# A graph attention layer on one core: program order throughout, half of the one-hot transposes by DMA, block loads on GpSimd's queue, the last scaling on ScalarE

## The chip, the cores and the metric

The kernel runs on one core of one Trainium2 chip. The metric is the device time of one execution in microseconds; before the change it is 372.82 us, the median of three runs (372.75 to 373.14).

## The reference

4096 nodes with 64 features, 50,000 directed edges, 4 heads, 64 output features per head. Cut to what matters:

```python
x_proj[h] = x @ weight[h]
score[h, e] = sum(x_proj[h, src[e]] * att_src[h]) + sum(x_proj[h, dst[e]] * att_dst[h])
score = where(score > 0, score, 0.2 * score)
output[h, dst[e]] += exp(score[h, e]) * x_proj[h, src[e]]      # for every edge
output[h, n] /= sum(exp(score[h, e]) for e with dst[e] == n) + 1e-8
return output.transpose(1, 0, 2).reshape(num_nodes, -1)
```

## The kernel before

The edges are first brought into order by two sorts on VectorE, so that afterwards each block of 121 destination nodes finds its edges in 16 groups of at most 128, one group for each sixteenth of the source nodes. Then 34 blocks are worked off, with one-hot matrices in place of gathers and scatters.

**First sort** (L529 to L546). The edges lie as 128 rows of 391. VectorE makes a key from source and destination, sorts the rows and then runs of 8 rows (`Sorter.rows`, `Sorter.runs`, nearly all of it L183), and SyncE stores the result to DRAM (`store`, L237). Beside it ScalarE counts with 16 Sign passes how many keys lie below each boundary (`below`, L245). `tables` (L298) stands behind the store: it loads x and the weights, transposes x on PE, multiplies it with the attention vectors (at_ps, L335), and keeps in `xa` each node's features and its attention terms, in `adb` the terms of the destinations. `bounds` (L251) adds up the counts on PE (L256) and turns them on VectorE (L258 and following) into the addresses at which the second stage reads.

**Second sort** (`group`, L286). GpSimd gathers runs from DRAM by these addresses (L283), VectorE sorts again, SyncE stores, `bounds` gives the addresses of the blocks' windows. `Windows` gathers them, five pieces of 8 blocks each, and `unpack` (L352) splits each piece on VectorE into destination and source index and writes both as bf16 to DRAM (`gat_bins`), two stores a piece on SyncE. `longest` finds the longest run of edges; at the very end of the program every engine loads the two lengths into registers (L559, L561) and branches on them (L563). With this input the branch's body doesn't run.

**Blocks** (`Blocks.run`, L454). For block b, in program order of one turn of the loop:

- `load(b+3)`, on SyncE: 1 MB, the indices of a block, the same for all 128 partitions. Three buffers.
- `weigh(b)`, VectorE: wv, the larger of the two exponentials (L433), and val = xs x wv (L437).
- `gather(b+1)`, PE: 48 products of one-hot matrices with `xa` and `adb`; ScalarE then takes the exponentials (ex, L410) and the features (xs, L412) out of PSUM.
- `turn(b+1)`, PE and ScalarE: 16 transposes of the destinations' one-hot matrix into PSUM (L425), two copies of 8 back to SBUF (Sb, L426).
- `onehot(b+2)`, VectorE: the block's indices compared with the partition number, two operations (L390, L391).
- `give(b-1)`: PE multiplies the sums with the weights (pf, L490), VectorE adds 1e-8, takes the reciprocal and scales (inv, res, L493 to L496), SyncE stores the result (L499).
- `scatter(b)`, PE: 48 products, for each of 16 groups two with val and one with wv, into acc; ScalarE copies acc (aT, L483).

Sb, the one-hots, val, ex, xs and wv have two buffers each; xps, acc and pf have one. Each engine, and each DMA queue, works in the order in which its instructions are issued. From L525 on this is the order of the program (`manual_schedule`); the setup ahead of it (L61 to L142) is ordered by the scheduler.

Of the kernel before, what the change touches and what calls it, by code (L numbers as in the profile page):

```python
# [9 lines left out]
P = 128  # L10
# [3 lines left out]
I32 = mybir.dt.int32  # L14
# [21 lines left out]
def kernel(ctx: ExitStack, tc: tile.TileContext, x: bass.AP, edge_index: bass.AP,  # L36
# [25 lines left out]


# [43 lines left out]
    pm8 = bits("pm8", 0, 7)  # L107
    goff = cst.tile([P, 1], F32)
# [167 lines left out]

    def fetch(pool, skey, start, n, to, what):
# [63 lines left out]
    NT = NR  # L341

    class Windows:
# [9 lines left out]
        def unpack(self, i):  # L353
# [7 lines left out]
            for k in range(2):  # L361
                nc.sync.dma_start(out=dataclasses.replace(bin_dram[8 * i, k],
                                                          ap=[[2 * NR * W2, 8], [W2, NR], [1, W2]]),
                                  in_=self.tb[:, i, k, :])

    class Blocks:
# [27 lines left out]
        def gather(self, b):  # L394
# [4 lines left out]
            xps = self.psx.tile([P, 4, 512], F32, name="xps")  # L399
            for t in range(NT):  # L400
                o = xps[:, t // 4, (t % 4) * XC:(t % 4) * XC + XC]
# [10 lines left out]
            S.copy(out=xs[:], in_=av(xps[:], 0, [512, 4], [XC, 4], [1, Din]))  # L412
            self.ex[b], self.xs[b] = ex, xs

        def turn(self, b):
# [5 lines left out]
            for q in range(2):  # L421
                sp = self.pss.tile([P, NT // 2, W2], BF16, name="sp")
                for i in range(NT // 2):
                    t = q * NT // 2 + i
                    T.transpose(out=sp[:, i, :], in_=oh[:, 0, t * W2:(t + 1) * W2], identity=identb[:])  # L425
                S.copy(out=Sb[:, q * NT // 2:(q + 1) * NT // 2, :], in_=sp[:])  # L426
            self.Sb[b] = Sb

        def weigh(self, b):
# [7 lines left out]
            V.tensor_tensor(out=av(val[:], 0, [Dout, H], [C, NT], [1, Din]),  # L437
                            in0=av(xs[:], 0, [0, H], [2, NT * Din // 2], [1, 2]),
                            in1=av(wv[:], 0, [2, H * NT], [0, Din // 2], [1, 2]), op=OP.mult)
            self.val[b] = val  # L440

        def scatter(self, b):

            val, wv, Sb = self.val.pop(b), self.wv.pop(b), self.Sb.pop(b)
            acc = self.psa.tile([P, CW], F32, name="acc")
            for t in range(NT):
                for k in range(2):
                    T.matmul(out=acc[:, k * P:(k + 1) * P], lhsT=val[:, t, k * P:(k + 1) * P], rhs=Sb[:, t, :],  # L448
                             start=(t == 0 and k == 0), stop=(t == NT - 1), skip_group_check=True)
                T.matmul(out=acc[:, C:CW], lhsT=Sb[:, t, :], rhs=av(wv[:], 2 * t, [2 * NT, H]), start=False,  # L450
                         stop=(t == NT - 1), skip_group_check=True)
            self.sink.take(b, acc[:])

        def run(self, between=lambda: None):  # L454
            for b in range(3):
                self.load(b)
# [3 lines left out]
            between()  # L460
# [12 lines left out]
    class Finish:  # L473
# [7 lines left out]
        def take(self, b, acc):  # L481
            aT = self.fp.tile([P, CW], F32, name="aT")
            S.copy(out=aT[:], in_=acc)  # L483
# [131 lines left out]
```

## Time and profile before

The profiled execution took 373.68 us, its span 371.9 us.

| stretch, us | what happens | VectorE busy, us |
|---|---|---|
| 0 to 20 | edges land, sort 1 begins | 14.51 |
| 20 to 73 | sort 1 | 50.12 |
| 73 to 90 | x and weights land, tables on PE | 0.00 |
| 90 to 120 | at_ps on PE, then bounds | 2.22 |
| 120 to 164 | sort 2 | 37.37 |
| 164 to 186 | windows, unpack, first block loads | 10.90 |
| 196 to 360 | blocks | 156.74 of 164 |

Over the span PE is busy 58%, VectorE 76%, ScalarE 44%, GpSimd 5%. A timeline row gives the start, the duration, the engine (with q: its queue of issues), the line, the operation and the tiles, and in brackets how long the engine was idle before it and what ended that. Durations of operations that follow each other overlap a little; the distance from start to start is what an engine spends on one.

### The profile page before, as it was taken

The numbers are of one execution on the slowest core, as the hardware profiler recorded it, in microseconds if no ns is written. First come the engines' busy times: TensorE is split into PE (matmuls) and PEld (weight loads), VectorE is DVE, ScalarE is ACT, GpSimd is POOL, SyncE is SP. The second block draws the span as 40 slices with busy tenths as digits, with TensorE's granted clock in tenths as the row PEclk, the third lists the DMA queues.
The fourth block names the chain that finished last, engine by engine and source line by source line (L and its number), as shares of the span: only waits on it lengthen the run. The fifth ranks groups of instructions, "written<-read, shape, count | busy, mean of one in ns | idle before, by whom it ended". The sixth has DMA issues, their size and how long they took to land.

```text
span 371.9 us, 9662 instructions
## 1 busy us (share of the span) xinstructions
PE 215.6 (58%) x4122; PEld 206.5 (56%) x4122; DVE 282.4 (76%) x584; ACT 164.3 (44%) x290; POOL 18.9 (5%) x40
## 2 busy tenths in 40 slices
PE   0000000029996000000399999999999999999990
PEld 0000000016996000000399999999999999999980
DVE  4999999700002599974599999999999999999970
ACT  1840000015000499600086666655765566656640
POOL 2820000000000200014000000000000000000000
PEclk9999999999555555555599999999999999999996
DMA  2000000050000100002866556655675567655410
GB/s 86 1 7 0 0 0 1 28 120 0 2 0 0 29 0 0 1 28 67 345 227 223 199 220 254 239 200 208 245 250 200 205 243 254 209 203 229 143 42 20
DMA packets 13550, 43.96 MB, mean 118 GB/s; under 512 B 3308, under 2 KB 8492, under 8 KB 9148
## 3 DMA queue, kind: packets, MB, share of 16 engines
q1 hardware_dynamic: 12556, 42.22, 32.1%
q0 software_dynamic: 704, 0.66, 0.7%
q8 instruction: 34, 0.56, 0.7%
q10 hardware_dynamic: 240, 0.40, 0.3%
q14 instruction: 16, 0.13, 0.1%
HBM read 38.22 MB, written 5.05 MB: 116 GB/s over the span
## 4 chain that ended last, share of the span: by engine, by line
DVE 60%; PE 25%; DMA 6%; issue 3%; ACT 2%; SPq 1%; POOL 1%; DVEq 0%; POOLq 0%
DVE val L437 14%; DVE sA L183 11%; DVE sB L183 10%; DVE oh L390 7%; PE at_ps L335 7%; PE acc L448 7%; DVE oh L391 4%; PE sp L425 3%; DVE res L496 3%; PE xps L403 3%; DMA wS<-in_weight_dram 2%; PE xps L405 2%; PE pf L490 1%; PE ps L330 1%; DMA bc<-gat_bins 1%
## 5 line engine op out<-in xcount | busy, mean ns | idle before, releaser
L437 DVE TENSOR_TENSOR val<-xs,wv 128x4096 bf16<-128x4096 bf16 x34 | 77.9, 2292 | 4.1 <-ACT xs L412 0.6
L448 PE MATMUL acc<-Sb,val 128*128 128x128 bf16 x1088 | 79.9, 217 | 1.2
L450 PE MATMUL acc<-wv,Sb 128*128 128x4 bf16 x544 | 76.0, 168 | 0.0
L448 PEld LDWEIGHTS <-val 128*128 128x128 bf16 x1088 | 67.2, 96 | 6.3 <-DVE val L437 6.1
L426 ACT COPY Sb<-sp 128x1024 bf16<-128x1024 bf16 x68 | 66.2, 1039 | 0.0
L403 PE MATMUL xps<-xa,oh 128*128 128x72 bf16 x544 | 53.9, 194 | 15.5 <-DVE oh L390 15.5
L403 PEld LDWEIGHTS <-oh 128*128 128x128 bf16 x544 | 50.3, 98 | 15.8 <-DVE oh L390 15.8
L405 PE MATMUL xps<-xa,oh 128*128 128x72 bf16 x544 | 53.7, 195 | 0.4 <-DVE oh L391 0.4
L407 PE MATMUL xps<-adb,oh 128*128 128x8 bf16 x544 | 52.8, 169 | 0.0
L450 PEld LDWEIGHTS <-Sb 128*128 128x128 bf16 x544 | 52.1, 96 | 0.0
L407 PEld LDWEIGHTS <-oh 128*128 128x128 bf16 x544 | 50.2, 97 | 0.0
L405 PEld LDWEIGHTS <-oh 128*128 128x128 bf16 x544 | 49.6, 96 | 0.6 <-DVE oh L391 0.6
L390 DVE TENSOR_SCALAR oh<-bc,pF 128x4096 bf16<-128x4096 bf16 x34 | 43.5, 1281 | 7.0 <-DMA bc<-gat_bins 7.0
L318 PE MATMUL ps<-ident,wS 64*128 64x64 f32 x2 | 0.7, 350 | 80.8 <-DMA wS<-in_weight_dram 80.8
L318 PEld LDWEIGHTS ps<-ident,wS 64*128 64x128 f32 x2 | 0.4, 178 | 80.8 <-issue 80.8
L183 DVE TENSOR_TENSOR sA<-sB 128x256 f32<-128x256 f32 (+2 forms) x108 | 39.7, 409 | 1.8
L410 ACT ACTIVATE ex<-xps 128x128 f32<-128x128 f32 x34 | 9.4, 277 | 65.1 <-PE xps L407 65.1
L183 DVE TENSOR_TENSOR sB<-sA 128x256 f32<-128x256 f32 (+2 forms) x100 | 36.8, 409 | 1.7
L425 PE MATMUL sp<-identb,oh 128*128 128x128 bf16 x544 | 36.6, 221 | 0.0
L258 DVE TENSOR_SCALAR cnt<-cnt_ps 128x17 f32<-128x17 f32 (+1 forms) x3 | 0.5, 180 | 44.8 <-PE cnt_ps L256 44.8
L412 ACT CAST xs<-xps 128x1024 bf16<-128x1024 f32 x34 | 34.2, 1007 | 0.0
L425 PEld LDWEIGHTS <-oh 128*128 128x128 bf16 x544 | 31.5, 99 | 0.0
(115 smaller groups left out, 295.9 us busy)
## 6 DMA issues: line engine op xcount, KB each, us to landing
bc<-gat_bins SPq DMA_DIRECT2D x34, 1024.0 KB
out_dram<-res SPq DMA_DIRECT2D x33, 121.0 KB
gat_sorted<-sA SPq DMA_DIRECT2D x2, 256.0 KB
eD<-in_edge_index_dram ACTq DMA_DIRECT2D x1, 390.0 KB
eS<-in_edge_index_dram SPq DMA_DIRECT2D x1, 390.0 KB
gat_bins<-tb SPq DMA_DIRECT2D x10, 32.0 KB
out_dram<-res SPq DMA_DIRECT2D x1, 103.0 KB
win<-gat_sorted,wi POOLq DMA_INDIRECT x5, 2.5
```

Of the source, the lines that this page charges most:

```text
L183: V.tensor_tensor(out=av(d[:], o, [2 * h, n], [1, h]), in0=av(s[:], 0, [2 * h, n], [1, h]), in1=av(s[:], h, [2 * h, n], [1, h]), op=op)
L335: T.matmul(out=ps[:, b, :], lhsT=xT[:, b * step:b * step + P], rhs=uv[:, k, :], start=(b == 0), stop=True, skip_group_check=True)
L390: V.tensor_scalar(out=oh[:, 0:2, :], in0=bc[:], scalar1=pF[:, 0:1], scalar2=None, op0=OP.is_equal)
L403: T.matmul(out=o, lhsT=oh[:, 1, e], rhs=xa[:, 2 * t, :], start=(t % 4 == 0), stop=False, skip_group_check=True)
L405: T.matmul(out=o, lhsT=oh[:, 2, e], rhs=xa[:, 2 * t + 1, :], start=False, stop=False, skip_group_check=True)
L407: T.matmul(out=o[:, Din:XC], lhsT=oh[:, 0, e], rhs=adb[:, b, :], start=False, stop=True, skip_group_check=True)
L412: S.copy(out=xs[:], in_=av(xps[:], 0, [512, 4], [XC, 4], [1, Din]))
L425: T.transpose(out=sp[:, i, :], in_=oh[:, 0, t * W2:(t + 1) * W2], identity=identb[:])
L426: S.copy(out=Sb[:, q * NT // 2:(q + 1) * NT // 2, :], in_=sp[:])
L437: V.tensor_tensor(out=av(val[:], 0, [Dout, H], [C, NT], [1, Din]), in0=av(xs[:], 0, [0, H], [2, NT * Din // 2], [1, 2]), in1=av(wv[:], 0, ...
L448: T.matmul(out=acc[:, k * P:(k + 1) * P], lhsT=val[:, t, k * P:(k + 1) * P], rhs=Sb[:, t, :], start=(t == 0 and k == 0), stop=(t == NT - 1 ...
L450: T.matmul(out=acc[:, C:CW], lhsT=Sb[:, t, :], rhs=av(wv[:], 2 * t, [2 * NT, H]), start=False, stop=(t == NT - 1), skip_group_check=True)
```

## The change

- `manual_schedule` is entered at the start, so that the setup too stands in program order.
- `tables` is called ahead of the first sort instead of behind its store.
- The run lengths are loaded into registers right after `longest`, by a helper `room`.
- `unpack` takes the queues for its two stores: SyncE and ScalarE for piece 0, ScalarE for the others. The loads of blocks 0 to 2 are issued right after piece 0; all pieces are unpacked before the blocks begin.
- Block loads are issued on GpSimd's queue.
- `turn`: groups 8 to 15 are transposed by one DMA transpose on SyncE, groups 0 to 7 on PE as before, with one copy.
- ex is written as bf16, doubled and in the order in which wv is written; wv then reads it without strides.
- `scatter` makes the 16 products with wv first, then those with val, half by half, and streams 121 columns instead of 128. The last block's val is made in two halves.
- The 1e-8 is added by ScalarE as it copies the sums; the last scaling is four ScalarE activations with the reciprocal as scale.

```diff
+    order = ExitStack()
+    order.enter_context(tc.manual_schedule())
...
+    eps = cst.tile([P, 1], F32)
+    V.memset(eps[:], 1e-8)
...
+    def room(k, n):
+        return nc.values_load(most[0:1, k:k + 1], min_val=0, max_val=RUN * n,
+                              skip_runtime_bounds_check_because="a count of a run's edges")
...
+    NP = NT // 2
+    AW = 2 * BD + H
...
-            for k in range(2):
-                nc.sync.dma_start(out=dataclasses.replace(bin_dram[8 * i, k],
...
+            for k, eng in enumerate(engs):
+                eng.dma_start(out=dataclasses.replace(bin_dram[8 * i, k], ap=[[2 * NR * W2, 8], [W2, NR], [1, W2]]),
...
-                nc.sync.dma_start(out=t[:], in_=dataclasses.replace(bin_dram[b], ap=[[0, P], [NT * W2, 2],
+                nc.gpsimd.dma_start(out=t[:], in_=dataclasses.replace(bin_dram[b], ap=[[0, P], [NT * W2, 2],
...
-            xps = self.psx.tile([P, 4, 512], F32, name="xps")
+            xps = self.psx.tile([P, NT, P], F32, name="xps")
...
-            ex = self.bp.tile([P, NT, 2 * H], F32, name="ex")
-            S.activation(out=ex[:], in_=av(xps[:], Din, [512, 4], [XC, 4], [1, 2 * H]), func=ACTF.Exp)
+            ex = self.bp.tile([P, 2, H, NT, 2], BF16, name="ex")
+            S.activation(out=av(ex[:], 0, [2, NT], [2 * NT, 2 * H], [1, 2]),
+                         in_=av(xps[:], Din, [P, NT], [1, 2 * H], [0, 2]), func=ACTF.Exp)
...
-            for q in range(2):
-                sp = self.pss.tile([P, NT // 2, W2], BF16, name="sp")
...
+            nc.sync.dma_start_transpose(out=Sb[:, NP:NT, :], in_=oh[:, 0, NP * W2:NT * W2])
+            sp = self.pss.tile([P, NP, W2], BF16, name="sp")
+            for t in range(NP):
+                T.transpose(out=sp[:, t, :], in_=oh[:, 0, t * W2:(t + 1) * W2], identity=identb[:])
+            S.copy(out=Sb[:, 0:NP, :], in_=sp[:])
...
-            V.tensor_tensor(out=wv[:], in0=av(ex[:], 0, [1, H], [2 * H, NT], [0, 2]),
-                            in1=av(ex[:], H, [1, H], [2 * H, NT], [0, 2]), op=OP.max)
+            V.tensor_tensor(out=wv[:], in0=ex[:, 0], in1=ex[:, 1], op=OP.max)
...
+            for h in range(0, H, n):
+                V.tensor_tensor(out=av(val[:], h * Dout, [Dout, n], [C, NT], [1, Din]),
...
             for t in range(NT):
-                for k in range(2):
-                    T.matmul(out=acc[:, k * P:(k + 1) * P], lhsT=val[:, t, k * P:(k + 1) * P], rhs=Sb[:, t, :],
...
+                T.matmul(out=acc[:, 2 * BD:AW], lhsT=Sb[:, t, :], rhs=av(wv[:], 2 * t, [2 * NT, H]), start=(t == 0),
                          stop=(t == NT - 1), skip_group_check=True)
+            for k in range(2):
+                for t in range(NT):
+                    T.matmul(out=acc[:, k * BD:(k + 1) * BD], lhsT=val[:, t, k * P:(k + 1) * P], rhs=Sb[:, t, 0:BD],
+                             start=False, stop=(t == NT - 1), skip_group_check=True)
...
-                self.weigh(b)
+                self.weigh(b, 2 if b == ND - 1 else 1)
...
-            S.copy(out=aT[:], in_=acc)
+            S.copy(out=aT[:, 0:2 * BD], in_=acc[:, 0:2 * BD])
+            S.activation(out=aT[:, 2 * BD:AW], in_=acc[:, 2 * BD:AW], func=ACTF.Identity, bias=eps[:, 0:1])
...
-            V.tensor_scalar(out=inv[:], in0=aT[:, C:CW], scalar1=1e-8, scalar2=None, op0=OP.add)
-            V.reciprocal(out=inv[:], in_=inv[:])
+            V.reciprocal(out=inv[:], in_=aT[:, 2 * BD:AW])
             res = self.fp.tile([P, H, Dout], F32, name="res")
-            V.tensor_tensor(out=res[:], in0=av(pf[:], 0, [Dout, H], [1, Dout]), in1=av(inv[:], 0, [1, H], [0, Dout]),
-                            op=OP.mult)
+            for h in range(H):
+                S.activation(out=res[0:BD, h, :], in_=pf[0:BD, h * Dout:(h + 1) * Dout], func=ACTF.Copy,
+                             scale=inv[0:BD, h:h + 1])
...
-            so.rows(1, EL)
-            store(skey1, so.runs())
-            tables(pr, pps, pp1)
+        tables(pr, pps, pp1)
+        so.rows(1, EL)
+        store(skey1, so.runs())
...
+        n1, n2 = room(0, EL), room(1, L)
     with ExitStack() as st:
         blocks = Blocks(st, Finish(st))
+        win.unpack(0, nc.sync, nc.scalar)
+        for b in range(3):
+            blocks.load(b)
+        for i in range(1, NI):
+            win.unpack(i, nc.scalar, nc.scalar)
+        blocks.run()
+    order.close()
```

## Rows read from the trace of the kernel before

**Rows 1.** Waits: engine, line, released by: us in total, times, longest.

```profile
DVE cnt L258 <- PE cnt_ps L256: 44.8, 1, 44.8
```

**Rows 2.** Timeline between the sorts: start us, us, engine, line, operation.

```profile
72.49 0.35 SPq L237 DMA_DIRECT2D gat_sorted<-sA  x1
...
116.60 1.03 PE L256 MATMUL cnt_ps<-sgn,sel 128*128 128x17 f32 x4
...
117.25 0.18 DVE L258 TENSOR_SCALAR cnt<-cnt_ps 128x17 f32<-128x17 f32 x1 [44.78 <-PE cnt_ps L256]
...
120.70 1.06 POOL L283 DMA_INDIRECT raw<-gat_sorted,wi  x1 [100.12 <-DVE wi L281]
```

**Rows 3.** The chain that ended last, by time: start us, us, what.

```profile
73.98 6.69 DMA wS<-in_weight_dram
```

**Rows 4.** The block stretch: busy us (operations) by engine, TensorE clock, DMA.

```profile
196.00:360.00 164.00, 162.32 (x3621) 157.15 (x3618) 156.74 (x219) 105.60 (x157) 0.00 (x0) 1.00 0.60 213
```

**Rows 5.** Timeline of VectorE over one block.

```profile
268.65 0.16 DVE L493 TENSOR_SCALAR inv<-aT 128x4 f32<-128x4 f32 x1
268.85 0.18 DVE L494 RECIPROCAL inv<-inv 128x4 f32<-128x4 f32 x1
269.12 0.42 DVE L496 TENSOR_TENSOR res<-pf,inv 128x256 f32<-128x256 f32 x1
269.46 0.28 DVE L433 TENSOR_TENSOR wv<-ex 128x128 bf16<-128x128 f32 x1
269.85 2.29 DVE L437 TENSOR_TENSOR val<-xs,wv 128x4096 bf16<-128x4096 bf16 x1
272.06 1.28 DVE L390 TENSOR_SCALAR oh<-bc,pF 128x4096 bf16<-128x4096 bf16 x1
273.25 0.75 DVE L391 TENSOR_SCALAR oh<-bc,pF 128x2048 bf16<-128x2048 bf16 x1
273.91 0.17 DVE L493 TENSOR_SCALAR inv<-aT 128x4 f32<-128x4 f32 x1
```

**Rows 6.** Timeline of PE over the same block.

```profile
265.34 1.05 PE L425 MATMUL sp<-identb,oh 128*128 128x128 bf16 x16
...
266.23 0.66 PE L490 MATMUL pf<-Wbd,aT 128*128 128x128 f32 x4
...
266.93 0.11 PEld L448 LDWEIGHTS <-val 128*128 128x128 bf16 x2 [0.23 <-DVE val L437]
...
269.15 0.19 PE L403 MATMUL xps<-xa,oh 128*128 128x72 bf16 x1
```

**Rows 7.** Timeline of the start.

```profile
9.15 0.27 DVE L86 TENSOR_SCALAR b_i<-pidx 128x1 int32<-128x1 int32 x3
...
11.40 0.35 DVE L173 TENSOR_TENSOR sB<-sA 128x196 f32<-128x196 f32 x1
...
22.38 0.28 ACT L300 CAST identb<-ident 128x128 bf16<-128x128 f32 x1
```

**Rows 8.** Timeline from the second sort's store to the first block loads.

```profile
163.61 0.34 SPq L237 DMA_DIRECT2D gat_sorted<-sA  x1
...
166.38 0.94 POOL L283 DMA_INDIRECT win<-gat_sorted,wi  x1 [43.23 <-DVE mxr L272]
...
169.96 5.25 SPq L362 DMA_DIRECT2D gat_bins<-tb  x8
...
175.65 1.28 SPq L382 DMA_DIRECT2D bc<-gat_bins  x3
```

**Rows 9.** Groups by line and shape: busy us, mean ns, idle before.

```profile
L426 ACT COPY Sb<-sp 128x1024 bf16<-128x1024 bf16 x68 | 66.2, 1039 | 0.0
...
L320 ACT COPY wT<-ps 128x64 f32<-128x64 f32 x2 | 0.4, 212 | 58.6 <-PE ps L318 58.5
```

**Rows 10.** Instructions on the tile most: duration ns min/median/max, first and last start.

```profile
L559 SPq TENSOR_LOAD <-most x1: 646/646/646, 364.1 to 364.1; - x1
...
L561 SPq TENSOR_LOAD <-most x1: 887/887/887, 364.9 to 364.9; - x1
```

More of the change, by code (lines that the diff above doesn't have):

```diff
@@ L444, in scatter, with run @@
             val, wv, Sb = self.val.pop(b), self.wv.pop(b), self.Sb.pop(b)
[L445 removed]
+            acc = self.psa.tile([P, AW], F32, name="acc")
             for t in range(NT):
[L447 to L450 removed]
+                T.matmul(out=acc[:, 2 * BD:AW], lhsT=Sb[:, t, :], rhs=av(wv[:], 2 * t, [2 * NT, H]), start=(t == 0),
                          stop=(t == NT - 1), skip_group_check=True)
+            for k in range(2):
+                for t in range(NT):
+                    T.matmul(out=acc[:, k * BD:(k + 1) * BD], lhsT=val[:, t, k * P:(k + 1) * P], rhs=Sb[:, t, 0:BD],
+                             start=False, stop=(t == NT - 1), skip_group_check=True)
             self.sink.take(b, acc[:])
[L454 to L456 removed]
+        def run(self):
             self.onehot(0)
@@ L459, in run @@
             self.turn(0)
-            between()
             self.onehot(1)
@@ L559 @@
-    n1 = nc.values_load(most[0:1, 0:1], min_val=0, max_val=RUN * EL,
-                        skip_runtime_bounds_check_because="a count of a run's edges")
-    n2 = nc.values_load(most[0:1, 1:2], min_val=0, max_val=RUN * L,
-                        skip_runtime_bounds_check_because="a count of a run's edges")
+    with tc.tile_pool(name="sort1", bufs=1) as so1, tc.tile_pool(name="pre", bufs=1) as pr, \
+            tc.tile_pool(name="pps", bufs=2, space=PSUM) as pps, \
+            tc.tile_pool(name="pp1", bufs=1, space=PSUM) as pp1:
+        sli = so1.tile([P, EL], I32)
+        tF = so1.tile([P, EL], F32)
+        uF = so1.tile([P, EL], F32)
+        key = so1.tile([P, L], F32)
+        so = Sorter(so1, key)
+        for t in (key, so.a[2]):
+            V.memset(t[:, EL:L], KPAD)
+        src = av(eS[:], 0, [2, EL])
+        dst = av(eD[:], 0, [2, EL])
+        sgn = below(so1, src, EL, nb1, NR, NR)
+        V.tensor_scalar(out=sli[:], in0=src, scalar1=SG - 1, scalar2=None, op0=OP.bitwise_and)
+        V.tensor_scalar(out=tF[:], in0=sli[:], scalar1=1.0 - N, scalar2=None, op0=OP.mult)
+        V.scalar_tensor_tensor(out=uF[:], in0=dst, scalar=float(SG), in1=tF[:], op0=OP.mult, op1=OP.add)
+        V.scalar_tensor_tensor(out=key[:, 0:EL], in0=src, scalar=float(N), in1=uF[:], op0=OP.mult, op1=OP.add)
+        tables(pr, pps, pp1)
+        so.rows(1, EL)
+        store(skey1, so.runs())
+        bounds(so1, pp1, sgn, NR, EL, [sel1[:, 0, :], sel1[:, 1, :]], off1, m16, NR, ws1, we1)
@@ new lines @@
+    with tc.tile_pool(name="sort2", bufs=1) as so2, tc.tile_pool(name="pp2", bufs=1, space=PSUM) as pp2:
+        group(so2, pp2, ws1[:])
+        win = Windows(cst, ws2[:])
+        longest(so2, pp2, ws1, we1, 0)
+        longest(so2, pp2, ws2, we2, 1)
+        n1, n2 = room(0, EL), room(1, L)
+    with ExitStack() as st:
+        blocks = Blocks(st, Finish(st))
+        win.unpack(0, nc.sync, nc.scalar)
[4 more added lines that the diff above has]
+        blocks.run()
@@ L571 @@
                     longest(so3, pp3, ws2, we2, 1)
-                m2 = nc.values_load(most[0:1, 1:2], min_val=0, max_val=RUN * L,
-                                    skip_runtime_bounds_check_because="a count of a run's edges")
+                m2 = room(1, L)
                 with tc.For_i(0, m2, W2):
@@ L577 @@
                         for i in range(NI):
-                            win.unpack(i)
-                        Blocks(st, Total(total)).run()
+                            win.unpack(i, nc.sync, nc.scalar)
+                        blocks = Blocks(st, Total(total))
+                        for b in range(3):
+                            blocks.load(b)
+                        blocks.run()
             with ExitStack() as st:
```

56 lines of the change are left out of this document (11 added, 45 removed).

## The prediction

> **What bounds the kernel now.** I read the list of waits first, then the timeline around the longest wait, then the timeline of one block in the middle, then start and end. The waits show one long idle stretch of VectorE: 44.8 us at L258, where the bounds of the first sort wait for the counting matmul [rows 1]. The timeline says why: the first sort's store is issued at 72.49 us, but `tables` stands behind the sort in the program, so its loads go out after that store, PE runs tables until about 116.6 us, VectorE resumes at 117.25 and GpSimd's first gather goes out at 120.70 [rows 2]. The loads themselves are the first part of it: the chain has 6.69 us of waiting for the weights, queued behind the 4096 pieces of 256 bytes of x [rows 3]. All that time VectorE, which carries both sorts and most of the end, stands still.
>
> From about 196 to 360 us the kernel runs 34 blocks at a fixed period. Over 164 us VectorE is busy 156.74, PE 162.32 and ScalarE 105.60; the DMA engines 0.60 of the time at 213 GB/s [rows 4]. The VectorE timeline has no gap in a block: 268.65 to 273.91 is 5.26 us, made of 0.81 (inv, reciprocal, res), 0.39 (wv), 2.21 (val), 1.19 and 0.66 (the two one-hots) [rows 5]. PE is nearly as full: transposes from 265.34, final products from 266.23, scatter from 266.93 after 0.23 us of waiting for val, the next gather at 269.15 [rows 6]. So VectorE sets the period, and PE stands 0.23 us behind it: a gain on one alone would be worth 0.23 us.
>
> **The change part by part.** All sums start from the profiled execution's 373.68 us (span 371.9 and 1.8 around it); the median of the runs is 372.82.
>
> *Tables ahead of the sort.* x and the weights are issued at once, PE and ScalarE do tables beside the sort. ScalarE first makes its sixteen Sign passes, which end at 22.38 us now [rows 7]; from the landing of the weights (73.98 + 6.69 = 80.67 [rows 3]) to the counting matmul at 116.60 [rows 2] it was 36 us, so tables end near 58 us, some 14 us before the sort does. The counting matmul is then done when VectorE asks. The whole wait goes: -44.8. What is late next is the sort's store: it takes 2.77 us from issue to the gather that it releases (163.61 to 166.38 in the second sort [rows 8]), and the bounds take 120.70 - 117.25 = 3.45 us to that same point [rows 2]; the store is covered by 0.7 us. If it were slower I would lose that much, not more.
>
> *Program order from the start.* Now the setup operations are interleaved with the sort's first steps, 9.15 to 11.40 us [rows 7]: 2.25 us of VectorE. In program order they stand ahead of the sort and run while the edges load. About half depend on the one before (0.2 us apart, as 268.65 and 268.85 [rows 5]), half don't (0.07, by the x3 rows of 9.15); 36 of them are some 4.5 us, and end about 0.4 us after the edges land. x, loading beside the edges, may cost 0.3. I take -1.6, between -2.3 and +0.5.
>
> *Start of the blocks.* Now SyncE issues eight stores from 169.96 for 5.25 us, and only then the first block loads at 175.65 [rows 8]; VectorE waits for the first of them. Afterwards the two stores of unpack 0 go out on two queues, and the loads stand behind GpSimd's five gathers (1.25 us apart from 166.38, so to about 172.6) and its two register loads. First load near 173.5, about 2 us earlier: -2.0 (0 to -4). The remaining eight stores go to ScalarE's queue at 5.25/8 = 0.66 us each; ScalarE has nothing else before the first gather. The register loads of the run lengths move here from the end; on VectorE they end before the first window lands.
>
> *The block period, VectorE.* inv goes (ScalarE adds eps while it copies), res goes to ScalarE, the reciprocal stays with nothing to wait for: of 0.81 us about 0.15 remain. wv reads bf16 side by side instead of float32 spread by a stride: 0 to 0.07 us less. 5.26 - 0.66 - 0.03 = 4.57.
>
> *The block period, PE.* Eight of sixteen transposes go: half of 266.23 - 265.34 = 0.89, so 0.45. The scatter streams 121 columns instead of 128 in 32 of its 48 products: 32 x 7 columns at 2.4 GHz, 0.09. The wait of 0.23 goes if val is early. 5.26 - 0.23 - 0.45 - 0.09 = 4.49. The two engines are again level; for their handshakes I add 0.08 and take 4.65 us.
>
> *The block period, ScalarE.* It was busy 105.60 us over 31 blocks, 3.4 each [rows 4]. One copy of Sb goes (1.04 [rows 9]); four scalings of 121x64 come, by the 128x64 copy from PSUM at 0.21 each 0.85; ex writes twice as much and aT becomes two operations, 0.3 together by the same short copy. 3.5 us of 4.65: covered. Its four scalings wait for the reciprocal, which stands behind the one-hots on VectorE; ScalarE's next work behind them is the copy of acc, which is due at the end of the scatter, so this wait has room.
>
> *The DMA transpose.* No row shows one. It moves 256 KB from SBUF to SBUF. Lower end: the store of the same size, 2.77 us [rows 8]. Upper end: if it is cut into pieces of 32 bytes, 8192 of them, at the pace of x's 4096 pieces (about 6.7 us [rows 3]), some 13.5 us. The row nearest in size and form is the store; beside a block load that takes its share I take T = 4.5 us. The DMA engines go from 0.60 busy to 0.60 x (1.38/1.12 MB) x (5.26/4.65), about 0.84: room left. What hides T: Sb and the one-hots have two buffers each, so the transpose of block b may start when the scatter of b-2 ends and is wanted at the scatter of b. But the wait that it adds closes a ring through SyncE's queue: transpose b ends, one-hot b+2 may overwrite its source (1.85 us), the reciprocal of b-1 stands behind it (0.2), ScalarE's four scalings (0.85), the output store on SyncE, and behind that, in order, transpose b+2. With handoffs this is T + 3.5 us in two blocks. It decides from T = 2 x 4.65 - 3.5 = 5.8 us on. At 4.5 it costs nothing.
>
> The Trainium skill ("VectorE: DVE Perf Modes", the three transpose paths) gives 1.31 us for one 128x128 transpose by DMA, and "DMA: Bandwidth & Descriptors" (latency and other measured facts) 261 GB/s or more for large ones, an estimated 1.0 us of data here. By these T would be near my lower end and the sum the same.
>
> *Block loads on GpSimd's queue.* By the nearest row an issue takes GpSimd 0.94 us [rows 8], and the engine has nothing else to do. A load may go as soon as one-hot b has released its buffer and is wanted three blocks later, so even 8 us of delay is covered. The instruction starts as the one-hots end, and then VectorE runs wv and val for 2.6 us; so I take 0. The range is 0 to 0.94 us in each block, if the issue should hold a one-hot (rival c). A rule speaks for that: the Trainium skill ("SBUF — State Buffer", who interferes with whom) has VectorE in its two-port modes and a GpSimd instruction shut each other out, the later waiting for the whole of the earlier, and names tensor_scalar, the one-hots' operation. No row before shows the two together; by the rule the sum is 304 if the issue falls beside val and 332 if it falls on the one-hots.
>
> *End.* The last val comes in halves and the scatter takes its two halves one after the other: of the 2.22 us of scatter behind val (266.93 to 269.15) 0.09 goes, the short products, 0.5, stand ahead, and half of the rest, 0.82, is left: -1.4. res as four scalings, 0.85 in place of the 0.42 of 269.12 [rows 5]: +0.4. SyncE's register loads after the last store, 0.65 and 0.89 us [rows 10], are gone from the end: -1.5.
>
> **Sum.** Period: 30 full blocks x 0.61 = 18.3, and 0.5 in the first two, which aren't at the period yet. 373.68 - 44.8 - 1.6 - 2.0 - 18.8 - 1.4 + 0.4 - 1.5 = 304.0. Against the median, 0.9 less; for the small terms that may fail I leave it at 304.
>
> **Rivals.** (a) *The transpose ring takes VectorE's place.* At T = 7 us the period is (7 + 3.5)/2 = 5.26 and the blocks gain nothing: 304 + 30 x 0.61 = 322. For it: T is unknown, and it shares the engines with loads that already hold 0.60. Against: the 2.77 us row. (b) *The ring makes the kernel slower.* The same ring decides against the whole gain when the period passes 6.95 us (30 x 2.3 = 69 us lost), that is from T = 10.4 us. At T = 11 us it is 7.25 and 304 + 78 = 382; at the upper end, 13.5, 8.5 and 420. For it speaks only x's slow small pieces. (c) *GpSimd and VectorE get in each other's way.* If GpSimd's issue of 0.94 us falls on the one-hots in each block and holds them, the period is 5.6 and the time 304 + 30 x 0.94 = 332. For it: one-hots are 1.85 of 4.65 us. Against: the load is released at their end, and 2.6 us of other work of VectorE follow. (d) *Tables isn't covered* because ScalarE's part comes late: it would have to lose another 14 us before it costs anything.
>
> **How the numbers follow.** Forecast, period 4.5 to 4.9: 0.62, own range 299 to 312. (a) with all periods from 4.9 to 5.6: 0.18. (c): 0.06. The ring between 5.6 and 6.95 us, 333 to 372: 0.06. (b): 0.08. About 0.2% (0.75 us) is what a measurement can tell from no change. Faster 0.91, same 0.01, slower 0.08. Below 298 the period would have to be under 4.5, which neither engine's sum allows unless the start gives more; the upper end stands at 334, which leaves out (b) and the slower rings.
>
> **What would show it.** VectorE's wait at L258 gone, and the gather after the first sort at 74 us. at_ps beside the sort. In a block: VectorE without gaps or PE without gaps, 4.5 to 4.7 us apart. If PE or VectorE waits for the DMA that writes Sb, or the one-hot waits for it, T is over 5.8 us and (a) or (b) holds. If one-hots last over 1.28 and 0.75 us, (c). The first block load at 175.65 - 46.4 - 2 = 127 us. The prediction is wrong if the period lies over 4.9.

## The result, and the profile after

The changed kernel takes 339.48 us (median of four runs, 337.26 to 369.86) against 372.98 us of the kernel before in the same rounds: a ratio of 0.907, interval 0.903 to 0.912. It is faster, as forecast, but by 33.5 us where 69 were forecast; 339.48 lies above 304.0 and above the range's end at 334. The execution that was profiled is one that ran longer, 369.86 us (span 368.0); what it shows of the blocks is checked below against profiles of other kernels.

Everything ahead of the blocks came as forecast. The timeline of the changed kernel (start, duration, engine, line, operation), lines that answer to [rows 2, 8]:

```profile
70.58 0.36 SPq L242 DMA_DIRECT2D gat_sorted<-sA  x1
...
73.92 1.05 POOL L293 DMA_INDIRECT raw<-gat_sorted,wi  x1 [58.75 <-DVE wi L291]
...
126.10 1.70 POOL L393 DMA_DIRECT2D bc<-gat_bins  x3 [0.73 <-issue]
...
131.81 1.29 DVE L401 TENSOR_SCALAR oh<-bc,pF 128x4096 bf16<-128x4096 bf16 x1 [3.64 <-DMA gat_bins<-tb]
...
138.29 2.29 DVE L449 TENSOR_TENSOR val<-xs,wv 128x4096 bf16<-128x4096 bf16 x1 [0.67 <-ACT xs L424]
```

The store is issued 1.91 us earlier (forecast 1.6), the first gather 46.8 (46.4), the first block loads 49.6 (48.4). The wait of [rows 1] is gone. The first val starts 48.2 us earlier; in the kernel before it stood here:

```profile
186.46 2.29 DVE L437 TENSOR_TENSOR val<-xs,wv 128x4096 bf16<-128x4096 bf16 x1 [0.61 <-ACT xs L412]
```

The waits have a new head (engine, line, what it waited for: us in total, times, longest):

```profile
DVE oh L401 <- DMA Sb<-oh: 62.2, 23, 13.3
...
PE acc L459 <- DMA Sb<-oh: 46.1, 16, 11.9
```

VectorE's next one-hot waits until the DMA transpose has read the one-hot of two blocks before, and PE's scatter waits for what the transpose writes: the sign that the prediction named for "T is over 5.8 us". "DMA Sb<-oh" is 33% of the chain. The windows of the blocks (length, then busy us and operations of PE, PEld, VectorE, ScalarE and GpSimd, TensorE's clock, DMA share, GB/s) answer to [rows 4]:

```profile
180.00:220.00 40.00, 32.86 (x750) 31.61 (x748) 29.30 (x32) 25.28 (x64) 3.59 (x7) 0.97 1.14 264
220.00:260.00 40.00, 36.34 (x788) 35.29 (x785) 32.44 (x39) 24.96 (x63) 3.76 (x7) 0.95 1.04 248
```

The DMA share, which adds up the times of packets and so can pass 1, is 1.04 to 1.14 instead of 0.60, while the bytes went up only from 213 to 248 and 264 GB/s. The page's list of DMA queues (packets, MB, share) says what is new: SyncE's queue carries 42340 packets, against 12556 with the block loads in it before.

```profile
q0 software_dynamic: 5600, 36.31, 33.3%
q1 hardware_dynamic: 42340, 15.18, 30.3%
```

The kernel with all transposes on PE (below) has 6436 there, so the 34 transposes are 35904 packets: 1056 each, 1024 of 256 bytes and 32 of 4. A block load is 144 packets. VectorE's own work in a block is as forecast; it only waits. The row of GpSimd (POOL) is a block load's issue:

```profile
235.28 1.29 DVE L401 TENSOR_SCALAR oh<-bc,pF 128x4096 bf16<-128x4096 bf16 x1 [1.26 <-DMA Sb<-oh]
236.48 0.75 DVE L402 TENSOR_SCALAR oh<-bc,pF 128x2048 bf16<-128x2048 bf16 x1
237.15 0.17 DVE L504 RECIPROCAL inv<-aT 128x4 f32<-128x4 f32 x1
237.23 0.20 DVE L444 TENSOR_TENSOR wv<-ex 128x128 bf16<-128x128 bf16 x1
...
237.53 0.54 POOL L393 DMA_DIRECT2D bc<-gat_bins  x1 [5.29 <-DVE wv L444]
...
237.56 2.29 DVE L449 TENSOR_TENSOR val<-xs,wv 128x4096 bf16<-128x4096 bf16 x1
242.35 1.29 DVE L401 TENSOR_SCALAR oh<-bc,pF 128x4096 bf16<-128x4096 bf16 x1 [2.50 <-DMA Sb<-oh]
```

### The profile page after: what moved, and what is told of

It reads as the page before. It is cut to its first block, busy times and chain, and to the rows that moved or that the text cites. A ratio compares the mean times of both kernels' runs of the same rounds, so it can differ in the third digit from the quotient of the medians.

```text
span 368.0 us, 9325 instructions
## 1 busy us (share of the span) xinstructions
PE 211.2 (57%) x3850; PEld 203.2 (55%) x3850; DVE 263.3 (72%) x518; ACT 170.4 (46%) x426; POOL 37.1 (10%) x74
## 3 DMA queue, kind: packets, MB, share of 16 engines
q1 hardware_dynamic: 42340, 15.18, 30.3%
## 4 chain that ended last, share of the span: by engine, by line
DMA 37%; DVE 29%; PE 22%; issue 7%; POOL 1%; ACT 1%; POOLq 0%; DVEq 0%; ACTq 0%
DMA Sb<-oh 33%; PE acc L463 12%; DVE sA L188 11%; DVE sB L188 10%; PE xps L414 4%; PE xps L416 3%; PE acc L459 2%; DMA bc<-gat_bins 2%; PE pf L501 1%; DVE sB L217 1%; DMA eS<-in_edge_index_dram 1%; POOL win L293 1%; PE sp L436 1%; DMA raw<-gat_sorted,wi 1%; DVE sA L178 1%
## 5 line engine op out<-in xcount | busy, mean ns | idle before, releaser
L449 DVE TENSOR_TENSOR val<-xs,wv 128x4096 bf16<-128x4096 bf16 (+1 forms) x35 | 78.0, 2231 | 6.7 <-ACT xs L424 2.9
L463 PE MATMUL acc<-Sb,val 128*128 128x121 bf16 x1088 | 73.0, 232 | 1.2 <-issue 1.2
L414 PE MATMUL xps<-xa,oh 128*128 128x72 bf16 x544 | 59.1, 198 | 15.4 <-DVE oh L402 14.8
L414 PEld LDWEIGHTS <-oh 128*128 128x128 bf16 x544 | 54.0, 104 | 13.9 <-DVE oh L401 13.9
L507 ACT ACTIVATE res<-pf,inv 121x64 f32<-121x64 f32 x136 | 31.7, 322 | 58.4 <-DVE inv L504 26.8
L418 PEld LDWEIGHTS <-oh 128*128 128x128 bf16 x544 | 53.1, 102 | 0.0
L416 PEld LDWEIGHTS <-oh 128*128 128x128 bf16 x544 | 50.7, 98 | 3.3 <-DVE oh L402 1.2
L459 PE MATMUL acc<-wv,Sb 128*128 128x4 bf16 x544 | 22.5, 169 | 46.6 <-DMA Sb<-oh 46.1
L459 PEld LDWEIGHTS <-Sb 128*128 128x128 bf16 x544 | 20.7, 97 | 48.9 <-DMA Sb<-oh 48.2
L421 ACT ACTIVATE ex<-xps 128x256 bf16<-128x256 f32 x34 | 13.3, 392 | 52.2 <-DMA bc<-gat_bins 29.3
L393 POOL DMA_DIRECT2D bc<-gat_bins x34 | 18.4, 542 | 180.8 <-DVE wv L444 171.8
L250 ACT ACTIVATE junk<-kr,nb 128x512 f32<-128x512 f32 x34 | 24.5, 722 | 24.5 <-DVE kr L301 23.4
L437 ACT COPY Sb<-sp 128x1024 bf16<-128x1024 bf16 x34 | 35.1, 1032 | 0.0
```

The costliest lines, as they stand in the source:

```text
L250: S.activation(out=junk[:], in_=v, func=ACTF.Sign, bias=nbnd[:, b:b + 1], scale=1.0, accum_out=sgn[:, b:b + 1])
L414: T.matmul(out=o, lhsT=oh[:, 1, e], rhs=xa[:, 2 * t, :], start=(t % 4 == 0), stop=False, skip_group_check=True)
L416: T.matmul(out=o, lhsT=oh[:, 2, e], rhs=xa[:, 2 * t + 1, :], start=False, stop=False, skip_group_check=True)
L418: T.matmul(out=o[:, Din:XC], lhsT=oh[:, 0, e], rhs=adb[:, b, :], start=False, stop=True, skip_group_check=True)
L437: S.copy(out=Sb[:, 0:NP, :], in_=sp[:])
L449: V.tensor_tensor(out=av(val[:], h * Dout, [Dout, n], [C, NT], [1, Din]), in0=av(xs[:], 0, [0, n], [2, NT * Din // 2], [1, 2]), in1=av(wv[ ...
```

## The experiments

The expectations use these theories. **T1**: the DMA engines have no room. In its form 1a a transpose's packets take their time on the engines whatever the queue; in 1b loads and transposes on two queues cost each other more than their sum; in 1c the transpose lands late because of the loads in flight. **T2**: the prediction's ring, a fixed time T from a transpose's issue to its landing, with room on the engines.

**e_again**: nothing is changed.

> The changed kernel once more, unchanged, to have it beside the others. Theory 1 (the DMA engines are the bound: a DMA transpose and the block loads beside it keep all 16 of them busy longer than the engines need for a block): 337 to 342 us, with stalls of uneven length from block to block. Theory 2 (the ring through SyncE's queue: transpose, one-hot, reciprocal, scaling, output store, next transpose; a constant latency T of some 7 to 8 us): 337 to 342 us too, but with an even period of about 5.6 us.

340.57 us (333.71 to 353.12; ratio 0.902). The distances from block to block are uneven, from 4.5 to over 15 us. A ring with a fixed T would give even ones.

**e_tables**: the kernel before, with `tables(pr, pps, pp1)` moved ahead of `so.rows(1, EL)` and no other edit.

> The kernel before with one part of the change alone: tables is called ahead of the first sort. The forecast's step says that the whole wait of 44.8 us goes and nothing else moves: 373.3 - 44.8 = 328.5 us. If tables beside the sort slowed the sort, or the store of the first sort became the next wait, it would be over 331.

329.03 us (328.71 to 329.45; 0.882): this edit alone gives 44 us, as the sum had it.

**e_noload**: the loads of blocks 3 to 33 are left out, the transposes stay.

```diff
+            if 3 <= b < ND:
+                self.bc[b] = self.kept[b % 3]
```

> Only the first three blocks' indices are loaded; the later blocks use these again (their loads are left out, the values of the output change with it). The DMA transposes stay. Theory 1: without the loads the transposes find the DMA engines free; the period falls to the engines' 4.5 us: 138.3 + 33 x 4.5 + 15.9 + 1.9 = 304.6 us. Theory 2: the latency of a transpose does not hang on the loads, the ring stays as it is: about 338 us.

304.17 us (303.76 to 304.80; 0.815): the forecast's figure. VectorE runs without a gap, 4.48 us a block, and never waits for Sb except for 0.5 us once. Its timeline, and its window:

```profile
203.91 1.28 DVE L404 TENSOR_SCALAR oh<-bc,pF 128x4096 bf16<-128x4096 bf16 x1
205.11 0.75 DVE L405 TENSOR_SCALAR oh<-bc,pF 128x2048 bf16<-128x2048 bf16 x1
205.77 0.17 DVE L507 RECIPROCAL inv<-aT 128x4 f32<-128x4 f32 x1
205.86 0.20 DVE L447 TENSOR_TENSOR wv<-ex 128x128 bf16<-128x128 bf16 x1
206.19 2.29 DVE L452 TENSOR_TENSOR val<-xs,wv 128x4096 bf16<-128x4096 bf16 x1
208.40 1.28 DVE L404 TENSOR_SCALAR oh<-bc,pF 128x4096 bf16<-128x4096 bf16 x1
```

```profile
180.00:220.00 40.00, 40.00 (x966) 39.90 (x964) 38.69 (x46) 31.57 (x81) 0.00 (x0) 1.00 0.57 87
```

So T by itself is short enough, the ring doesn't bind, and T2 as it stands falls: the transposes cost time only beside the loads. Counted in the traces from the start of a transpose's issue to the end of its last packet, T is 2.4 us here (the median of the 34) and 6.7 us, up to 18.5, in the changed kernel's profile.

**e_pe_all**: all sixteen groups by PE, in two halves with two copies. **e_pe_sp**: the same, and the loads on SyncE's queue.

```diff
-            nc.sync.dma_start_transpose(out=Sb[:, NP:NT, :], in_=oh[:, 0, NP * W2:NT * W2])
+            for q in range(2):
...
+                S.copy(out=Sb[:, q * NP:(q + 1) * NP, :], in_=sp[:])
```

> All 16 groups are transposed on PE and copied by ScalarE, as before the change; the rest of the change stays. Both theories: the stalls on Sb and on the one-hots go. PE then needs 4.49 + 0.45 = 4.94 us a block and sets the period. From the trace of the changed kernel: first val at 138.3 us, 33 periods of 4.95, 15.9 us from the last val to the end of the span, 1.9 around it: 319 us. If something else of the change (loads on GpSimd's queue, scaling on ScalarE) cost the time, it stays near 338.

> All transposes on PE, block loads on SyncE's queue: what the change of queue alone is worth. Loads are three blocks ahead in either queue, and PE sets the period of 4.95 us: 317.9 us within 1. If GpSimd's descriptors or VectorE's one-hots held each other up, this would be faster by a few us.

317.89 us (317.28 to 318.63; 0.852, interval 0.850 to 0.854) and 317.56 (317.49 to 318.48; 0.851, 0.849 to 0.853). These are the fastest complete kernels of the study. The DMA transpose, meant to relieve PE, costs 22 us against doing without it. With all transposes on PE, the queue of the loads makes no difference.

**e_outq**: the output stores on ScalarE's queue (`nc.scalar.dma_start(out=out[...`). **e_buf3**: `pool(name="blk", bufs=3)` instead of 2.

> The output stores are issued by ScalarE instead of SyncE, so that no transpose stands behind a store that waits for the scaling. Theory 2: the ring is cut; what is left in two blocks is T and one scatter, some 1.0 us less than before, so 0.5 us a block: about 320 us. Theory 1: the DMA engines have the same work, 335 to 342 us.

> The pool that holds one-hots, Sb, xs, ex, wv and val gets three buffers instead of two, so that a transpose has one block more time. Theory 2 (latency): the wait goes, 4.6 us a block: 138.3 + 33 x 4.6 + 17.8 = 308 us. Theory 1a and 1b (the DMA engines are full): the average can't fall, 332 to 342 us; only the unevenness is smoothed.

368.0 us (355.92 to 384.93) and 361.24 (340.08 to 379.21). Both open the ring of the prediction, one at the store and one at the one-hots, and neither comes near the 320 and 308 us that the ring theory gives. With the stores on ScalarE's queue all four runs are above those of e_again, which no theory had said; with the third buffer the runs spread too far for that, and the shortest, 340.08, is the changed kernel's time. In both profiles single blocks take up to 16 and 17 us, as in the changed kernel's own (17.75 and 14.39). What brings this about wasn't tried.

**e_spload**: the loads on SyncE's queue, so that loads, transposes and stores share one.

> Block loads are issued by SyncE again, in one queue with the transposes and the output stores. By the share of the 16 engines that each queue's packets take, a block load alone takes 2.9 us (kernel without DMA transposes), the transpose alone 1.9 (kernel without the later loads), the rest of a block 0.3: 5.1 us a block if nothing is lost by mixing; in the changed kernel the two together take 3.5 + 2.5. Theory 1a (the engines are simply full, in any order): 335 to 342 us, as the changed kernel. Theory 1b (packets of a transpose and of a load that alternate on an engine slow each other): in one queue they stand behind each other, the period falls to 5.1: 138.3 + 33 x 5.1 + 17.8 = 324 us. Theory 2 (latency of the ring): about 340, or more, since the loads now stand in the ring's queue.

332.92 us (330.44 to 333.85; 0.890). The longest block is now 7.38 us, so the long stalls don't come with one queue, but the mean is still (316.40 - 137.66) / 33 = 5.42. 1b's 324 and 1a's 335 both miss by a little.

**e_bc2**: two buffers for the block loads instead of three.

> Two instead of three buffers for the block loads, which so run ahead by two blocks instead of three; queues as in the changed kernel. Theory 1c (a transpose in its own queue shares the engines packet by packet with all loads already queued in the other, whose packets are far larger, and so ends after them; the stalls of 10 to 17 us are transposes that wait for three to five loads): the stalls get shorter, to 6 to 9 us, and the time falls to 326 to 335 us. If the number of queued loads has nothing to do with it, the time stays at 334 to 345 or grows because loads come late.

343.23 us (335.69, 340.74, 345.71 and 353.79; 0.919). In its profile, of the run of 335.69 us, the longest block is 7.24 us: the sign of 1c came, which speaks for the queued loads as the cause of the long stalls. The time didn't come: the mean block is still 5.43 us, so the long stalls aren't the main cost.

**e_dma4**, **e_dma4_sp**, **e_dma2_sp**: four or two groups by DMA instead of eight, the others by PE with two copies; in the last two with the loads on SyncE's queue.

> Only 4 of the 16 groups go by DMA, 12 by PE with two copies. PE needs 4.49 + 0.22 = 4.71 us a block. DMA: 2.9 for the load, 0.9 to 1.2 for the transpose, 0.3 else: 4.1 to 4.4. Theory 1a: PE sets the period, 138.3 + 33 x 4.75 + 17.8 = 313 us. Theory 1b: the mixing still costs, 4.9 to 5.2 us a block, 318 to 328 us. Theory 2 (latency of a transpose is mostly fixed): stays above 330.

> 4 of 16 groups by DMA and the block loads on SyncE's queue. PE 4.71 us a block; DMA 2.9 + 1.0 + 0.3 = 4.2 in one queue. Theory 1b and 1c (what hurts is the two queues beside each other): 4.75 us a block, 138 + 33 x 4.75 + 17.8 = 313 us, which would be less than the 317.9 of the kernel with all transposes on PE. Theory 1a with losses in any order: 320 to 328 us.

> Two of sixteen groups by DMA, fourteen by PE with two copies, block loads on SyncE's queue. PE's period is 4.95 us with none by DMA and 4.48 with eight, so 4.83 here: if transposes of 64 KB and loads merely add up on the DMA engines (2.45 + 0.34 us + stores), the time is 317.6 - 34 x 0.12 = 314 us, under the 317.56 of the kernel with all sixteen on PE. If even small transposes cost the loads beside them more than their own time and land late, as the time of 327.59 us with four groups says, it is 319 us or more.

328.13 us (324.66 to 330.36), 327.59 (325.28 to 331.05) and 326.88 (324.28 to 328.51; 0.877, interval 0.875 to 0.880). A quarter of the packets still costs 9 us against none. Against the time that the engines would allow, two groups cost 13 us (326.88 against the 314 of the expectation) and eight, on one queue, 29 (332.92 against 304.17): much of a transpose's cost doesn't go with its amount.

**e_micro**: in place of the blocks 24 transposes alone, 24 loads alone, and 24 of each together on their two queues. **e_micro_sp**: in place of the blocks 24 pairs on one queue, then 24 on two.

> The blocks are left out (the output is zeros); in their place 24 DMA transposes of 128x1024 alone, then 24 block loads of 1 MB from GpSimd's queue alone, then 24 of each together, with 8 and 6 buffers so that the queues stay full. Theory 1a and 1b: transposes alone 1.9 us apart, loads alone 2.9; together 4.8 (1a, the sum) or 5.5 and more (1b). Theory 2: a transpose takes 6 us or more even alone, or together no more than the slower of both, 2.9.

> Leaves out the 34 blocks: zeros are stored as output. After the windows and one block's one-hots come 24 pairs of a block load (1 MB) and a 256 KB DMA transpose, once with the loads on SyncE's queue, the one the transposes are on, and once more with the loads on GpSimd's queue. Alone a load took 2.45 us and a transpose 1.35 us, so 3.80 us a pair without a loss; with two queues 4.74 us a pair were measured. If the loss and the bunched landing come from two queues that share the DMA engines, the first half takes 3.8 to 4.0 us a pair, lands evenly, and the second half 4.7 with waits of 13 us or more. If the loss belongs to a transpose's small packets beside any load, both halves take 4.6 to 4.8 us a pair.

Alone a transpose goes every 1.35 us (161.83 to 171.26, seven intervals; 193 GB/s) and a load every 2.45 us (426 GB/s). Within one transpose the packets follow each other without a pause: the window from 162.80 to 164.05 us holds all 1056 of one; some 0.3 us pass before the next one starts.

```profile
DMA packets 1056, 0.26 MB, mean 210 GB/s; under 512 B 1056, under 2 KB 1056, under 8 KB 1056
```

On two queues a pair takes 4.74 us, a quarter over the sum. e_micro_sp repeats that in its second half (253.13 to 327.98, 16 pairs: 4.68); in its first half, on one queue, a pair takes 3.37 (158.15 to 208.71, 15 pairs), less than the sum. Its timeline of VectorE, which waits for load and transpose in turn (L492 and L493), first on one queue, then on two:

```profile
178.38 0.17 DVE L492 TENSOR_TENSOR gate<-gate,mB 128x16 bf16<-128x16 bf16 x1 [2.25 <-DMA mB<-gat_bins]
179.27 0.17 DVE L493 TENSOR_TENSOR gate<-gate,mS 128x16 bf16<-128x16 bf16 x1 [0.72 <-DMA mS<-oh]
181.76 0.17 DVE L492 TENSOR_TENSOR gate<-gate,mB 128x16 bf16<-128x16 bf16 x1 [2.33 <-DMA mB<-gat_bins]
182.62 0.17 DVE L493 TENSOR_TENSOR gate<-gate,mS 128x16 bf16<-128x16 bf16 x1 [0.70 <-DMA mS<-oh]
...
267.54 0.17 DVE L493 TENSOR_TENSOR gate<-gate,mS 128x16 bf16<-128x16 bf16 x1 [14.04 <-DMA mS<-oh]
268.19 0.17 DVE L493 TENSOR_TENSOR gate<-gate,mS 128x16 bf16<-128x16 bf16 x1 [0.28 <-DMA mS<-oh]
269.05 0.17 DVE L493 TENSOR_TENSOR gate<-gate,mS 128x16 bf16<-128x16 bf16 x1 [0.50 <-DMA mS<-oh]
270.10 0.17 DVE L493 TENSOR_TENSOR gate<-gate,mS 128x16 bf16<-128x16 bf16 x1 [0.68 <-DMA mS<-oh]
...
288.26 0.17 DVE L493 TENSOR_TENSOR gate<-gate,mS 128x16 bf16<-128x16 bf16 x1 [17.79 <-DMA mS<-oh]
```

On two queues a transpose lands after 14 to 18 us, and then four of them within 3 us. That is 1b, and it fits the long blocks of the changed kernel. But on one queue loads and transposes would fit: 3.37 us of 4.5. Why then does e_spload take 5.42? The next runs test one answer: the prediction's ring with T near 7.3 (2 x 5.42 - 3.5), since there a transpose stands behind a load of 2.45 us.

**e_first**: one queue, and the transpose ahead of the load. **e_first_out**: besides, the output stores on GpSimd's queue. **e_first_buf3**: e_first with three `blk` buffers. **e_first_deep**: e_first with five buffers for the loads, issued five blocks ahead (`self.load(b + 5)`).

```diff
-                self.load(b + 3)
                 self.weigh(b, 2 if b == ND - 1 else 1)
                 self.gather(b + 1)
                 self.turn(b + 1)
+                self.load(b + 3)
```

> One queue: block loads on SyncE's queue as in e_spload, and in program order the load of b+3 now stands behind the transpose of b+1 instead of ahead of it, so that a transpose no longer queues behind 1 MB of load (2.45 us). Ring theory (the prediction's ring, 2P = T + 3.5, with T about 7.3 to 7.9 us in e_spload because the load goes first): T falls by some 2.4 us to 5.0 to 5.5, the ring asks for 4.3 to 4.5 us, PE and VectorE set the period again and the time is 304 to 312 us. If it is not order in the queue but the throughput of the DMA engines with small packets, nothing changes: 330 to 334 us.

> As e_first, and the output stores go on GpSimd's queue: no store that waits for res stands ahead of a transpose any more, so the ring through res is open. Ring theory: 303 to 308 us. But if a second queue beside the transposes is enough for the bunched, late landing, even with 121 KB a block in it, it is worse than e_first: 320 us or more, with waits for Sb of over 10 us.

> As e_first, with three buffers for Sb, the one-hots, val, ex, xs and wv: the wait of the one-hot for the transpose two blocks back becomes one for three blocks back, the ring asks 3P = T + 3.5 plus a little. Ring theory: 303 to 308 us, no waits for Sb left. If the throughput of the DMA engines bounds it, 330 us as in e_spload.

> As e_first (loads on SyncE's queue, each behind a transpose), with five buffers for the block loads instead of three, and a load issued five blocks ahead. In e_first no wait for Sb was left; the one-hots waited for the block loads instead, each of which was issued behind a transpose that itself waits for the scatter before, and landed some 7 us later. In e_first_out's trace the DMA engines moved about 4 us of data in a block of 5.4 and stood still for the rest. Latency theory (what costs is the wait from issue to landing in rings of two or three blocks, not the amount): with loads two blocks earlier no wait for loads or Sb is left and the time is 304 to 312 us. Throughput theory (loads and transposes together hold the engines for 5.4 us a block, whatever the order): 325 to 345 us, the waits for loads stay.

343.98 us (0.921, interval 0.919 to 0.923), 334.54 (0.894, 0.887 to 0.901), 347.5 (0.923, 0.921 to 0.926) and 330.22 (0.878, 0.871 to 0.884). The ring theory's 303 to 312 us failed four times. T, counted as above, is 6.3 us in e_spload and 3.4 in e_first (medians); with 3.4 the ring would ask for 3.5 us a block, and e_first took 5.75. Opening the ring at the store did help against e_first (343.98 to 334.54), but only back to the time of e_spload. The waits of VectorE's one-hot in e_spload, in e_first and in e_first_deep:

```profile
DVE oh L401 <- DMA Sb<-oh: 28.8, 29, 2.8
```

```profile
DVE oh L401 <- DMA bc<-gat_bins: 37.6, 23, 4.6
```

```profile
DVE oh L401 <- DMA Sb<-oh: 19.4, 17, 5.3
...
DVE oh L401 <- DMA bc<-gat_bins: 4.0, 2, 3.4
```

With the transpose first, the waits for it are gone and the loads are late; with the loads deep, the transposes are late again. The order only chooses which transfer is late. What does not go away is seen when the windows of e_first_deep are cut along the transfers of one block (columns as above):

```profile
206.30:209.30 3.00, 3.00 (x80) 3.00 (x79) 3.00 (x4) 1.10 (x5) 0.00 (x0) 1.00 0.90 347
209.30:209.90 0.60, 0.60 (x15) 0.60 (x12) 0.11 (x2) 0.36 (x2) 0.00 (x0) 1.00 3.46 239
209.90:211.10 1.20, 1.20 (x30) 1.19 (x29) 0.46 (x2) 1.20 (x3) 0.00 (x0) 1.00 0.15 15
211.10:211.60 0.50, 0.24 (x5) 0.13 (x3) 0.50 (x1) 0.50 (x1) 0.00 (x0) 1.00 1.98 464
211.60:214.60 3.00, 2.86 (x75) 2.85 (x75) 3.00 (x3) 1.50 (x7) 0.00 (x0) 1.00 0.90 332
```

A load at 347 GB/s; then the first half of the transpose (some 500 packets); then 1.2 us in which the queue moves 15 GB/s; then the second half and the next load. The DMA share of 3.46 at the start of the pause says that packets which began there lasted through it. The changed kernel shows the same, in the block whose VectorE rows stand in the section on the result (235.28 to 242.35):

```profile
237.50:238.00 0.50, 0.50 (x23) 0.50 (x20) 0.44 (x1) 0.50 (x3) 0.47 (x1) 1.00 4.76 226
238.00:240.00 2.00, 2.00 (x50) 1.89 (x45) 1.85 (x1) 1.79 (x6) 0.06 (x1) 1.00 0.41 66
240.00:243.50 3.50, 1.23 (x27) 1.23 (x28) 1.15 (x1) 1.16 (x2) 0.00 (x0) 1.00 0.99 316
```

In e_noload most transposes run through without a pause, as at 200 us, but not all, as at 218:

```profile
200.00:200.60 0.60, 0.60 (x10) 0.59 (x8) 0.60 (x1) 0.60 (x2) 0.00 (x0) 1.00 0.97 223
200.60:201.20 0.60, 0.60 (x22) 0.60 (x20) 0.60 (x2) 0.60 (x2) 0.00 (x0) 1.00 0.97 214
...
218.00:218.60 0.60, 0.60 (x10) 0.59 (x8) 0.60 (x2) 0.60 (x2) 0.00 (x0) 1.00 3.51 199
218.60:220.85 2.25, 2.25 (x55) 2.25 (x53) 2.12 (x5) 2.25 (x6) 0.00 (x0) 1.00 0.68 15
220.85:221.40 0.55, 0.55 (x25) 0.55 (x22) 0.55 (x1) 0.52 (x3) 0.00 (x0) 1.00 1.05 227
```

There 13 of the 34 pause, for 0.6 to 2.4 us, and it costs nothing: with the pause a transpose's packets take at most 3.3 us of a block's 4.48, and nothing else wants the engines.

So in the block of e_first_deep above the engines need 1.1 us for the transpose's halves, 1.2 for the pause and 3.0 for the load: 5.3 us. The mean of its blocks is (313.65 - 137.85) / 33 = 5.33, and from 150 to 300 us there are packets in flight for 148 of the 150 us. The DMA engines are the bound, though for a fifth of that time they move next to nothing.

**What stays open.** What brings the pause about. It needs neither loads (e_noload) nor the blocks' work: on one queue in e_micro_sp there is none from 157 to 211 us, but the first transposes ahead of that have pauses of up to 1.75 us, one of them in this window, in which PE, VectorE and ScalarE do nothing:

```profile
149.10:150.60 1.50, 0.00 (x0) 0.00 (x0) 0.00 (x0) 0.00 (x0) 0.00 (x0) 0.50 1.35 30
```

During the pause in this window, and beside 12 of the 13 pausing transposes of e_noload (the first has block loads beside it), a packet of an instruction queue (q8 or q14 in the page's list of queues) is in flight, as this line of that list for e_noload from 218.6 to 220.9 us shows; of the 15 transposes there that have no such packet beside them none pauses for over 0.5 us.

```profile
q8 instruction: 1, 0.02, 2.5%
```

That is a coincidence in time which no run tested, and in e_first_deep 4 of 25 pauses lack it. Why two queues land transposes by fours, no run tells either.

## Why the prediction was wrong

Against e_noload's profile (span 302.1) the terms can be set side by side. Up to the first val: 186.46 to 138.20, -48.3 (forecast -48.4). From there to the last val: 171.0 to 148.5, -22.5 (forecast -18.8, mainly because 4.65 us was taken and 4.48 came). From the last val to the end of the span: 14.4 to 15.4, +1.0 (forecast -2.5). Two errors of 3.5 to 3.7 us cancel; that 304.17 so nearly meets 304.0 is partly luck.

- *Tables, program order, start of the blocks*: right, each within 1.2 us. The cover named for the register loads at the start held as well.
- *Block period*: right, and the margin of 0.08 for handshakes, with which 4.57 became 4.65, was not needed. PE and VectorE both run without a gap, PE 40.00 of 40 us busy.
- *ScalarE covered*: right; 31.57 of 40 us is 3.5 us in a block.
- *Block loads on GpSimd's queue*: 0 was right, and rival (c) did not come about. GpSimd's issue of a load lasts 0.54 us and falls beside val in 28 of 34 cases, as at 237.53; val takes 2.29 us as before. Only one issue met a one-hot, which took 1.32 us in place of 1.29. The rule of the Trainium skill that was weighed there ("SBUF — State Buffer", who interferes with whom: the two engines shut each other out) shows no cost in this trace, but an issue that falls on the one-hots block after block, the case that (c) priced, was not seen.
- *End*: wrong by 3.5 us, in two places. The register loads are gone from the end ([rows 10] stand at 118.9 and 119.9 us in the profile after), but in e_noload the span ends 8.0 us after the last store's issue, where it was 7.8 (8.4 in the changed kernel's profile): the 1.5 us didn't go. What takes their time wasn't tried. Nor did the halves of the last val bring their 1.4: from that val to the last aT are 5.1 us where there were 4.7. PE doesn't wait for val there. It still has the block before to finish and its final products, which wait for aT, so the last scatter starts at 289.40 us, after both halves:

```profile
286.70 2.36 DVE L452 TENSOR_TENSOR val<-xs,wv 128x2048 bf16<-128x2048 bf16 x2 [0.67 <-ACT xs L427]
...
288.87 0.70 PE L504 MATMUL pf<-Wbd,aT 128*121 128x128 f32 x4 [0.51 <-ACT aT L496]
...
289.40 0.56 PE L462 MATMUL acc<-wv,Sb 128*128 128x4 bf16 x16
```

- *The DMA transpose*: **this step failed**. "At 4.5 it costs nothing" held without the loads, as e_noload shows, with T at 2.4 us; beside them T was 6.7, over the limit of 5.8. The sentence that gave it room, "about 0.84: room left", scaled the busy share of 0.60 with the bytes. A transpose is 1056 packets, not 256 KB of a load: alone it moves 193 GB/s where loads move 426, and in the blocks its pause brings it to 2.3 us of the engines. Load, transpose and pause are 5.3 us a block, over the 4.48 that PE and VectorE need, and that is 28 us in 33 blocks; with one queue the kernel is 28.8 us over e_noload (332.92 against 304.17; 26 with the loads deep, 330.22). The two queues with their bunches add another 4 to 6 (ratios of 0.902 and 0.907 against 0.890). Together they are about the 35 us that were missing.

Rival (a) named the place, VectorE's one-hot waiting for the transpose through SyncE's queue; its price of 322 us was too low, and 339.48 fell where the prediction had given the ring a chance of 0.06 (333 to 372). The mechanism was another: not a fixed T in a ring, since no kernel that opened the ring came near the time that the ring asks for, and in the changed kernel's profile the ring with T = 6.7 would take 5.1 us a block, where the mean is (352.15 - 138.29) / 33 = 6.48. The Trainium skill ("DMA: Bandwidth & Descriptors", latency and other measured facts) gives 261 GB/s or more for transposes by DMA; the run with transposes alone has 193 back to back, the 0.3 us between them included; the measurement decides. But the loads beside it, which no such figure covers, made the difference.

## What to carry to other kernels

Size a DMA by its packets and by what is in flight beside it, not by its bytes: if a new transfer shares the engines with loads that already hold 0.60 of them, run it alone, then beside them, before it is called free. Small transposes by DMA next to a steady stream of loads are better left on PE as long as PE's price (here 4.95 - 4.48 = 0.47 us a block) is below that delay; and if they must be, one queue for both was better here by 1 to 2% with eight groups (0.890 against 0.902 and 0.907) and the same with four (327.59 and 328.13). When each reordering only changes which transfer is late, the engines behind the queues are the bound, and a window cut along single transfers shows it.

## What the runs showed of the hardware

- A DMA transpose of 128x1024 bf16 from SBUF to SBUF is 1024 packets of 256 bytes and 32 of 4. Back to back one goes every 1.35 us, with some 0.3 us between two; in the blocks most of them pause about halfway, in the windows shown for 1.2 to 2.25 us, without loads (e_noload) 13 of 34.
- Pairs of a 1 MB load and such a transpose: 3.37 us on one queue, 4.7 us on two, there with transposes landing four at a time after 13 to 20 us.
- With the output stores on ScalarE's queue the changed kernel took 355.92 to 384.93 us in four runs, without that edit 333.71 to 353.12 in the same round; why, no run tells.
